# Experts split by token count: short ones in four 32-column tiles, the rest in two 64-column tiles

## The chip, the core and the metric

The kernel runs on one core of a Trainium2 chip. The metric is the device time of one execution in microseconds. The core has TensorE (matmuls; the profile's PE, its weight loads PEld), VectorE (DVE), ScalarE (ACT), GpSimd (POOL) and SyncE (SP), which here issues nearly all transfers from device memory to the on-chip memory.

## The reference, cut to what matters

One layer of a block for 256 latent tokens of width 1024. Its first half (a modulated input projection, three token mixers, a merge) is not touched. The second half is a mixture of 32 experts, of which each token uses 4:

```python
logits = (h @ w_router + b_router)                 # 256 x 32
top_val, top_idx = lax.top_k(logits, 4)
probs = softmax(top_val)                           # weight of a token at its experts
for each expert:
    gate, up = split(h @ w_gate_up + b_gate_up)    # 1024 -> 1024 and 1024
    gate = minimum(gate, 7); up = clip(up, -7, 7)
    y = ((up + 1) * gate * sigmoid(1.702 * gate)) @ w_down + b_down
    out += combine[:, expert, None] * y
```

and at the end a layer norm. All is float32. The weights of one expert are 12.6 MB, of all 403 MB.

## The kernel before, in words

**First part** (to about 310 us): the mixers, the merge, the router. It counts each expert's tokens into `cnt`, and the place of each token at each expert into `posq`.

**Experts.** The loop `for e in range(NE)` (L1479 to L1552) is unrolled in the program. For each expert 64 slots are filled: `select` (VectorE) makes the 0/1 matrix of tokens and slots, for two experts at a time, and `gather` (TensorE, then ScalarE) multiplies by it and writes the chosen tokens, transposed, into `hT`, half of the width at a time. `gate_up` (L1388) multiplies `hT` (64 columns, the stationary side) with 512 columns of weights at a time; two 64-column tiles of TensorE, `pg[0:64]` and `pg[64:128]`, work side by side. Each such float32 matmul is two matmul instructions in the profile. The columns of the weights are laid out in two halves (`hf`): the first half of gate and up is multiplied for all of the width (L1489), then `act` (L1395, five operations, four of them on VectorE) makes the gated product, while TensorE goes on with the second half (L1509, L1512). `spots` (L1373) makes the matrix `sT` that puts results back to their tokens, and the weights of the slots. `turn` (L1403) transposes the product, `down` (L1410) multiplies with the down weights, in two parts with a `turn` and a `gather` between. `spread` scales the result and splits it into a high and a low part, and `scatter` (L1421) adds both to the sums `acc` with `sT`; this happens in the next expert, after its first half of gates (L1492). `biases` writes the bias into a bank before the matmuls add to it, by a matrix `bse` that is copied from `bsel`.

**More than 64 tokens.** `cnt[e]` is loaded into a register of TensorE, VectorE and ScalarE. Two blocks under `tc.If(tv > SLOTS)` follow: `rest_gate` (L1503) does the first half for slots 65 to 128, with the gate weights still in place, and `rest` (L1518) all of the others. A block under `tc.If(most > 2 * SLOTS)` (L1557), behind the last expert, handles more than 128 tokens, which doesn't occur with these inputs. Where the condition is false the engine jumps over the block.

**Transfers.** `queue` holds all weights in order: for each expert four pieces of gate and up (`gu`) and two of down (`dn`), 2048 KB each; the last expert's down weights come in four of 1024 KB. On chip there are slots for nine pieces of 2048 KB. `pump` (L148) issues the queue's head on SP as soon as the text has a free slot; `done(key)` frees a slot and pumps. At run time the transfer waits on SP until the last reader of the slot that stands in the text before it is past. `done` of gate pieces 0 and 1 stands behind the block L1503, of 2 and 3 behind the block L1518, and of the down pieces each behind its part of `down`.

**End.** `stats3` and `norm2` (L1575 to L1600) normalise the sums and write four blocks of output. One of these goes through ScalarE and GpSimd (L1592 to L1594), and ScalarE issues its transfer (L1595).

The functions that the diff touches, with the line numbers of the profile:

Of the kernel before, what the change touches and what calls it, by code (L numbers as in the profile page):

```python
# [21 lines left out]
P = 128  # L22
# [95 lines left out]
def kernel(ctx, tc, x, cx, cols, rows, csts, wsm, wgt, bada, brt, sgub, bdn, bgu,  # L118
# [21 lines left out]
    for e in range(NE):  # L140
        queue += [(("gu", e, i), wgu[e, i]) for i in range(4)]
        if e < NE - 1:
            queue += [(("dn", e, i), wdn[e, i]) for i in range(2)]
        else:
            queue += [(("dn1", e, i), wdn[e, i // 2][:, 2048 * (i % 2):2048 * (i % 2) + 2048]) for i in range(4)]
    loaded = {}

    def pump():  # L148
        while queue:
# [11 lines left out]
            nc.sync.dma_start(out=s, in_=src)  # L161
# [63 lines left out]
    with ExitStack() as p1:  # L225
# [1058 lines left out]
        bsel = Buf(A2, NE, 2)  # L1284
# [20 lines left out]
        G.memset(bsel[:], 0.0)  # L1305
        for r in range(4):
            S.copy(out=bsel[32 * r:32 * r + 32, :, r % 2], in_=ident[32 * r:32 * r + 32, 32 * r:32 * r + 32])
# [33 lines left out]
    for t in range(2):  # L1341
        mm(ps[0:1, 64:64 + NE], ones[:, 0:1], sel[:, t], start=t == 0, stop=t == 1)


    def chunk():
        return dict(sT=Buf(R, 256), cwv=Buf(A2, 2), gT=Buf(A2, KB, SLOTS), gc=[Buf(A2, 256)])

    yhx, ylx = Buf(R, 512), Buf(R, 512)
    cur, over = chunk(), chunk()
    over["gc"] = over["gc"] + cur["gc"]  # L1350
    cur["gc"] = cur["gc"] + [Buf(A2, 256)]
    ysum = Buf(A2, 512)
    up, sg = ysum[:, 0:256], ysum[:, 256:512]
    sw = ysum[:, 0:256].rearrange("p (t a n) -> p t a n", t=2, a=2)
# [18 lines left out]
    def spots(b, sl, e):  # L1373
        for t in range(2):
            V.tensor_scalar_mul(sw[:, t], sl[:, t, :].unsqueeze(1).to_broadcast([P, 2, SLOTS]), cw[:, t, e:e + 1])
        pw = sps2()
        for t in range(2):
            T.transpose(pw[:, P * t:P * t + P], sw[:, t].rearrange("p a n -> p (a n)"), ident[:])  # L1378
# [3 lines left out]
    def bias_of(e):  # L1382
        V.tensor_copy(out=bse[e % 2][:].rearrange("p (q n) -> p q n", q=2), in_=bsel[:, e, :].unsqueeze(2).to_broadcast([P, 2, SLOTS]))  # L1383

    def biases(e, hf, pg):
        mm(pg[:], bse[e % 2][:], bst[:, hf, :], start=True, stop=False, skip_group_check=True)  # L1386

    def gate_up(hT, pg, ks, w):  # L1388
        for k in ks:
            wk = w[k // 2].rearrange("p (k n) -> p k n", k=2)  # L1390
            for q in range(2):
                mm(pg[64 * q:64 * q + 64, :], hT[:, k, :], wk[:, k % 2, 512 * q:512 * q + 512], start=False, stop=k == KB - 1,  # L1392
# [288 lines left out]
```

## Time and profile before

| | |
|---|---|
| median of 3 runs | 1283.39 us (1281.62 to 1283.76) |
| the profiled execution | 1286.55 us, of which the span is 1284.7 |
| TensorE busy | 1189.9 us |
| VectorE busy | 461.2 us |
| ScalarE busy | 284.5 us |
| moved from device memory | 468.92 MB |

A page of the profile shows busy time per engine and, in 40 slices, the share of busy time, the clock that TensorE was granted (1.00 is full speed) and the rate of the transfers. Times in the views count from the start of the span. "Idle before" is the time that the engine stood still ahead of an instruction, and behind the arrow stands what ended it; `PEq` is TensorE's sequencer, which runs branches and waits.

### The profile page before, as it was taken

The numbers are of one execution on the slowest core, as the hardware profiler recorded it, in microseconds if no ns is written. First come the engines' busy times: TensorE is split into PE (matmuls) and PEld (weight loads), VectorE is DVE, ScalarE is ACT, GpSimd is POOL, SyncE is SP. The second block draws the span as 40 slices with busy tenths as digits, with TensorE's granted clock in tenths as the row PEclk, the third lists the DMA queues.
The fourth block names the chain that finished last, engine by engine and source line by source line (L and its number), as shares of the span: only waits on it lengthen the run. The fifth ranks groups of instructions, "written<-read, shape, count | busy, mean of one in ns | idle before, by whom it ended". The sixth has DMA issues, their size and how long they took to land. (4 is left out here: it accounts for less than half of the span.)

```text
span 1284.7 us, 16504 instructions
## 1 busy us (share of the span) xinstructions
PE 1189.9 (93%) x6619; PEld 611.3 (48%) x6624; DVE 461.2 (36%) x988; ACT 284.5 (22%) x548; POOL 28.3 (2%) x42
## 2 busy tenths in 40 slices
PE   7997999999999999999999999999888999889884
PEld 5897889995333434334433334333333333333321
DVE  6488768796222222222212221222222122212223
ACT  5352745634111111111111111111111111111101
POOL 1000000002000000000000000000000000000000
PEclk9998999998999999999999999999999999999998
DMA  9745648777999999989959999999999999999993
GB/s 389 274 152 204 232 178 296 294 311 297 392 415 427 424 427 427 427 323 429 375 213 387 428 425 427 427 425 427 427 426 426 427 425 427 425 427 426 428 423 149
DMA packets 39470, 471.74 MB, mean 367 GB/s; under 512 B 4529, under 2 KB 4657, under 8 KB 7473
## 3 DMA queue, kind: packets, MB, share of 16 engines
q1 hardware_dynamic: 37008, 463.75, 87.3%
q10 hardware_dynamic: 1696, 4.40, 1.0%
q8 instruction: 89, 1.46, 0.5%
q0 software_dynamic: 640, 1.84, 0.5%
q14 instruction: 37, 0.30, 0.1%
HBM read 468.92 MB, written 1.05 MB: 366 GB/s over the span
## 5 line engine op out<-in xcount | busy, mean ns | idle before, releaser
L1392 PE MATMUL bank<-arena,arena 128*64 128x512 f32 x1808 | 408.8, 596 | 18.3 <-DMA arena<-in_wgu_dram 17.7
L1414 PE MATMUL bank<-arena,arena 128*64 128x512 f32 x1088 | 251.7, 604 | 25.5 <-DMA arena<-in_wdn_dram 17.9
L1392 PEld LDWEIGHTS bank<-arena,arena 128*64 128x64 f32 x1808 | 124.1, 137 | 260.5 <-issue 235.6
L1414 PEld LDWEIGHTS bank<-arena,arena 128*64 128x64 f32 x1088 | 79.3, 138 | 174.8 <-issue 152.7
L246 PE MATMUL bank<-rounded 128*128 128x256 f32 (+1 forms) x1152 | 149.6, 289 | 0.1
L246 PEld LDWEIGHTS bank<-rounded 128*128 128x128 f32 x1152 | 144.0, 195 | 1.8 <-issue 0.6
L1397 DVE TENSOR_SCALAR arena<-bank 128x256 f32<-128x256 f32 x68 | 28.9, 424 | 280.4 <-PE bank L1392 280.4
L1417 DVE SCALAR_TENSOR_TENSOR arena<-bank,arena,g2q 128x512 f32<-128x512 f32 x33 | 24.8, 751 | 271.8 <-PE bank L1414 163.3
L1398 ACT ACTIVATE arena<-arena 128x256 f32<-128x256 f32 x68 | 28.4, 417 | 366.5 <-DVE arena L1397 362.6
L1407 ACT COPY arena<-bank 128x256 f32<-128x256 f32 x68 | 25.3, 372 | 294.4 <-PE bank L1406 294.4
L1392 PE MATMUL bank<-arena 128*64 128x512 f32 x368 | 85.4, 606 | 3.0 <-DMA arena<-in_wgu_dram 2.6
L343 DVE TENSOR_TENSOR rounded<-arena,rounded 128x2048 fp32r<-128x2048 f32 x29 | 66.2, 2284 | 15.1 <-ACT rounded L338 15.1
L1367 PE MATMUL bank<-arena 128*128 128x128 f32 (+1 forms) x576 | 69.9, 275 | 0.7 <-DVE rounded L1383 0.7
L1367 PEld LDWEIGHTS bank<-arena 128*128 128x128 f32 x576 | 66.9, 192 | 1.5 <-ACT arena L1232 0.8
L1370 ACT ACTIVATE arena<-bank,shc 128x128 f32<-128x128 f32 (+1 forms) x144 | 53.3, 450 | 50.7 <-PE bank L1367 50.7
L338 ACT CAST rounded<-arena 128x2048 fp32r<-128x2048 f32 x29 | 55.0, 1898 | 9.2 <-PE bank L246 5.6
L1379 DVE TENSOR_SCALAR rounded<-bank 128x256 fp32r<-128x256 f32 x34 | 14.5, 425 | 117.0 <-PE bank L1378 117.0
L1392 PEld LDWEIGHTS bank<-arena 128*64 128x64 f32 x368 | 25.2, 139 | 53.6 <-issue 45.3
L1418 ACT CAST rounded<-arena 128x512 fp32r<-128x512 f32 x33 | 20.4, 618 | 111.5 <-DVE arena L1417 111.5
L1426 PE MATMUL bank<-rounded 64*128 64x512 f32 x264 | 40.8, 418 | 3.6 <-ACT rounded L1418 3.1
L1426 PEld LDWEIGHTS bank<-rounded 64*128 64x128 f32 x264 | 22.8, 184 | 33.9 <-issue 25.1
L1386 PE MATMUL bank<-rounded 128*128 128x512 f32 x68 | 32.5, 477 | 5.8 <-PEq L1503 3.8
(326 smaller groups left out, 889.5 us busy)
## 6 DMA issues: line engine op xcount, KB each, us to landing
arena<-in_wgu_dram SPq DMA_DIRECT2D x128, 2048.0 KB, 28.7
arena<-in_wdn_dram SPq DMA_DIRECT2D x62, 2048.0 KB, 27.3
arena<-in_win_dram SPq DMA_DIRECT2D x23, 1024.0 KB, 5.3
arena<-in_wada_dram SPq DMA_DIRECT2D x16, 1024.0 KB, 4.9
arena<-in_wad_dram SPq DMA_DIRECT2D x8, 1024.0 KB, 11.1
arena<-in_wbr_dram SPq DMA_DIRECT2D x4, 1024.0 KB, 5.6
arena<-in_wout_dram SPq DMA_DIRECT2D x4, 1024.0 KB, 5.5
arena<-in_wdn_dram SPq DMA_DIRECT2D x4, 1024.0 KB, 33.6
```

The source lines that it names most:

```text
L246: mm(o, l, r, start=start and n == 0, stop=stop and n == len(todo) - 1)
L338: S.copy(out=wh[:, 0:2048], in_=w)
L343: V.tensor_tensor(out=wl[:, 0:2048], in0=w, in1=wh[:, 0:2048].bitcast(F32), op=ALU.subtract)
L1367: mm(pg[:, w * k:w * k + w], h2[:, t, 512 * a + P * k:512 * a + P * k + P], b["sl"][:, t].rearrange("p i n -> p (i n)"), start=t == 0, sto ...
L1370: S.activation(out=b["hT"][:, 4 * a + k].rearrange("p i n -> p (i n)"), in_=pg[:, w * k:w * k + w], func=AF.Identity, scale=shc[:, 1, 4 * ...
L1386: mm(pg[:], bse[e % 2][:], bst[:, hf, :], start=True, stop=False, skip_group_check=True)
L1392: mm(pg[64 * q:64 * q + 64, :], hT[:, k, :], wk[:, k % 2, 512 * q:512 * q + 512], start=False, stop=k == KB - 1, skip_group_check=True)
L1397: V.tensor_scalar_min(gc[:], pg[:, 0:256], LIMIT)
L1398: S.activation(out=sg[:], in_=gc[:], func=AF.Sigmoid, scale=SW_ALPHA)
L1407: S.copy(out=b["gT"][:, 4 * hf:4 * hf + 4, :].rearrange("p (q j) n -> p j q n", q=2), in_=pt[:, 0:256].rearrange("p (j q n) -> p j q n", j ...
L1414: mm(py[64 * q:64 * q + 64, :], b["gT"][:, k, :], wk[:, k % 2, 512 * q:512 * q + 512], start=k == 0, stop=k == KB - 1)
L1426: mm(acc[t][hf][:], b["sT"][sl, P * t:P * t + P], y_[sl, :], start=False, stop=last and y_ is ylx, skip_group_check=True)
```

## The change

- **Weights by input block.** The gate and up weights of an expert are laid out so that each piece holds two blocks of 128 inputs, and each block all 2048 columns, as four quarters of 256 gate and 256 up columns. Before, a piece held one half of the columns for four blocks.
- **Branch per expert.** `by_count` puts the gate part and the down part each under `tc.If(tv > FEW)` with an else, FEW being 32; expert 0 always takes the wide side without a branch.
- **Short side.** `gate_up` puts 32 slots on four 32-column tiles, one quarter of the columns on each, 512 wide, all into one bank; one `act` follows instead of two, and one `turn`. `down` uses the four tiles for two halves of the output and two of the input; the two input halves are added by `scatter`, whose matrix `sT` has the 32 slots four times.
- **Wide side.** `gate_up_wide` does both halves for the first four input blocks, then both for the rest, into two banks. `spots` and both `act` come after it.
- **Order.** All gates of an expert now stand ahead of `scatter` of the expert before, of both overflow blocks and of the gathers; the down part comes last, in one go. `done` of all four gate pieces stands behind the second overflow block, `done` of both down pieces behind the down part.
- **Overflow.** The first block gathers and does the first half of the input blocks, the second block all the rest, down and scatter included. They have banks and buffers for both halves.
- **Biases.** `biases2` writes the bias for either case into the bank ahead of the branch, through two matrices whose content depends on the count; they are made once by small operations on GpSimd.
- **More than 128 tokens.** `many` stands before the last expert and loads the weights again.
- **Last expert and end.** Its last gate piece and its last down piece come in smaller transfers, and the output block of GpSimd is issued by SP instead of ScalarE.

The core of the diff (removed functions and small renames are left out):

```diff
-        queue += [(("gu", e, i), wgu[e, i]) for i in range(4)]
+        queue += [(("gu", e, i), wgu[e, i]) for i in range(4 if e < NE - 1 else 3)]
...
+            queue += [(("gu1", e, i), wgu[e, 3][:, 2048 * i:2048 * i + 2048]) for i in range(2)]
...
+            if key == ("dn1", NE - 1, 3):
+                for i in range(2):
+                    nc.sync.dma_start(out=s[:, 1024 * i:1024 * i + 1024], in_=src[:, 1024 * i:1024 * i + 1024])
...
+    for r in range(4):
+        for t in range(2):
+            mm(ps[32 * r:32 * r + 32, 128:129], sel[:, t], ones[:, 0:1], start=t == 0, stop=t == 1)
...
+    def biases2(e, pg):
+        biases(e, 0, pg)
+        mm(pg[:], bsx[e % 2][:], bst[:, 1, :], start=False, stop=False, skip_group_check=True)
+    def gate_up(hT, pg, w):
+        for k in range(KB):
+            for r in range(4):
+                mm(pg[FEW * r:FEW * r + FEW, :], hT[:, k, 0:FEW], w[k][:, 512 * r:512 * r + 512], start=False, stop=k == KB - 1,
+                   skip_group_check=True)
+    def gate_up_wide(hT, pgs, ks, w, between=None):
+        for hf in range(2):
+            if hf and between:
+                between()
+            for k, wk in zip(ks, w):
+                for q in range(2):
+                    mm(pgs[hf][64 * q:64 * q + 64, :], hT[:, k, :], wk[:, 1024 * hf + 512 * q:1024 * hf + 512 * q + 512], start=False,
+                       stop=k == KB - 1, skip_group_check=True)
+    def down(b, py, w):
+        for i in range(4):
+            for h in range(2):
+                for q in range(2):
+                    mm(py[64 * q + FEW * h:64 * q + FEW * h + FEW, :], b["gT"][:, 2 * i + h, 0:FEW],
+                       w[i][:, D * h + 512 * q:D * h + 512 * q + 512], start=i == 0, stop=i == 3)
...
+        def gates(small):
+            shares(sl[:, :, 0:FEW] if small else sl, e)
+            if small:
+                gate_up(hT, g0, w)
+            else:
+                gate_up_wide(hT, [g0, g1], range(4), w, lambda: biases(e, 1, g1))
+                gate_up_wide(hT, [g0, g1], range(4, KB), w[4:])
+            pw = spots()
+            act(cur["gc"][0], g0)
+            places(cur, pw)
+            if not small:
+                act(cur["gc"][1], g1)
+        def downs(small):
+            turn(cur, 0, 4 if small else 2)
+            (down if small else down_wide)(cur, g0, wd)
+        by_count(gates)
+        if 0 < e < NE - 1:
+            scatter(prev, yx)
...
         with tc.If(tv > SLOTS):
-            rest_gate(e, w)
+            over_begin(e, 1, [g0, g1])
+            for hf in range(2):
+                biases(e, hf, (g0, g1)[hf])
+            over_gates([g0, g1], range(4), w)
+        if e % 2 == 0 and e + 2 < NE:
+            select(q_["sl"][:], 2, 0, e + 2)
+        if e % 2 == 0 and e + 2 < NE:
+            gather(q_, 0, 2)
         with tc.If(tv > SLOTS):
-            rest(e, g1, wu, wd)
+            over_gates([g0, g1], range(4, KB), w[4:])
+            over_end([g0, g1])
+            turn(over, 0)
+            py = sps2()
+            down_wide(over, py, wd)
+            spread(over, py, yx)
+            scatter(over, yx)
+        if e % 2 and e + 1 < NE:
+            gather(q_, 1, 2)
+        for key in [("gu", e, i) for i in range(4)] if not last else [...]:
+            done(key)
...
+            bias_of(e + 1)
+        if e + 2 < NE:
+            biases2(e + 1, g1)
+        by_count(downs)
+        for key in [("dn", e, i) for i in range(2)] if not last else [("dn1", e, i) for i in range(4)]:
             done(key)
...
-    S.dma_start(out=out[0:P, 512:1024], in_=o[0][1])
     stats3(1, 1)
     norm2(0, 0)
+    nc.sync.dma_start(out=out[0:P, 512:1024], in_=o[0][1])
...
-    gu = gu.transpose(0, 5, 1, 3, 2, 6, 4, 7).reshape(NE, 4, 2, P, 2048).transpose(0, 1, 3, 2, 4).reshape(NE, 4, P, 4096)
+    gu = A(w_gate_up)[0].reshape(NE, 4, 2, P, 2, 4, 256).transpose(0, 1, 3, 2, 5, 4, 6).reshape(NE, 4, P, 4096)
```

## Rows read from the trace of the kernel before

**Rows 1.** Page, transfer rate in 40 slices of 32.1 us.
```profile
GB/s 389 274 152 204 232 178 296 294 311 297 392 415 427 424 427 427 427 323 429 375 213 387 428 425 427 427 425 427 427 426 426 427 425 427 425 427 426 428 423 149
```

**Rows 2.** Windows: start:end length, engines' busy us (instructions), PEclk, DMA share, GB/s.
```profile
316.00:324.00 8.00, 7.84 (x39) 2.47 (x37) 3.81 (x12) 2.70 (x4) 0.00 (x0) 1.00 0.24 63
...
330.00:384.00 54.00, 51.22 (x250) 20.36 (x251) 12.97 (x34) 7.16 (x18) 0.00 (x0) 0.97 1.00 414
...
550.00:584.00 34.00, 33.53 (x174) 14.02 (x173) 6.65 (x17) 5.57 (x14) 0.00 (x0) 1.00 0.84 329
...
628.00:644.00 16.00, 15.51 (x72) 5.12 (x70) 5.21 (x14) 1.47 (x4) 0.00 (x0) 1.00 0.72 280
...
644.00:700.00 56.00, 53.27 (x255) 20.41 (x253) 11.43 (x27) 7.60 (x18) 0.00 (x0) 0.97 0.75 294
...
700.00:1254.00 554.00, 509.29 (x2475) 195.46 (x2471) 126.58 (x323) 69.21 (x168) 0.00 (x0) 1.00 1.01 426
```

**Rows 3.** Waits of SP's queue: us in total, times, longest.
```profile
SPq L161 <- PEq L1503: 200.5, 29, 12.8
...
SPq L161 <- PEq L1518: 166.2, 28, 7.5
```

**Rows 4.** Timeline of SP: start us, us, engine line op out<-in.
```profile
321.34 0.33 SPq L161 DMA_DIRECT2D arena<-in_wgu_dram  x1
```

**Rows 5.** DMA issues from 321.2 to 321.5: KB each, us to landing.
```profile
arena<-in_wgu_dram SPq DMA_DIRECT2D x1, 2048.0 KB, 7.7
```

**Rows 6.** Timeline of TensorE, expert 3; in brackets idle before, and releaser.
```profile
397.19 7.04 PE L1392 MATMUL bank<-arena,arena 128*64 128x512 f32 x32
...
404.16 1.20 PE L1426 MATMUL bank<-rounded 64*128 64x512 f32 x8
...
405.52 0.47 PE L1386 MATMUL bank<-rounded 128*128 128x512 f32 x1 [0.17 <-PEq L1503]
...
414.06 3.65 PE L1414 MATMUL bank<-arena,arena 128*64 128x512 f32 x16 [0.31 <-PEq L1518]
...
417.92 1.95 PE L1367 MATMUL bank<-arena 128*128 128x128 f32 x16
...
423.52 1.89 PE L1392 MATMUL bank<-arena 128*64 128x512 f32 x8
```

**Rows 7.** Timeline of TensorE, first instructions of experts 10 and 11.
```profile
612.38 3.60 PE L1392 MATMUL bank<-arena 128*64 128x512 f32 x16
...
671.14 1.45 PE L1392 MATMUL bank<-arena,arena 128*64 128x512 f32 x5
```

**Rows 8.** Timeline of TensorE at 17 us: 128x32 column tiles.
```profile
17.00 1.07 PE L260 MATMUL bank<-arena 128*32 128x256 f32 x16 [0.92 <-ACT arena L298]
```

**Rows 9.** Timeline of VectorE: one activation of a gate half.
```profile
1248.19 0.42 DVE L1397 TENSOR_SCALAR arena<-bank 128x256 f32<-128x256 f32 x1 [7.32 <-PE bank L1392]
...
1249.63 0.42 DVE L1401 SCALAR_TENSOR_TENSOR arena<-arena 128x256 f32<-128x256 f32 x1
```

**Rows 10.** Timeline of all engines, the tail.
```profile
1262.76 3.65 PE L1414 MATMUL bank<-arena,arena 128*64 128x512 f32 x16 [0.46 <-ACT arena L1407]
...
1267.27 1.99 PE L1444 MATMUL bank<-arena,rounded 64*128 64x512 f32 x8 [0.85 <-DVE arena L1543]
...
1271.19 1.29 DVE L1576 BATCH_NORM_STATS2 st<-bank 128x6 f32<-128x512 f32 x2 [3.97 <-PEq L1557]
...
1275.10 1.61 DVE L1584 SCALAR_TENSOR_TENSOR arena<-arena,rsx 128x512 f32<-128x512 f32 x1
...
1278.27 0.29 ACT L1579 ACTIVATE rsx<-mvx,lneps 128x1 f32<-128x1 f32 x1 [3.86 <-POOL arena L1594]
```

**Rows 11.** DMA issues from 1234.6 to 1234.8: the last weights.
```profile
arena<-in_wdn_dram SPq DMA_DIRECT2D x1, 1024.0 KB, 29.4
```

**Rows 12.** Timeline of TensorE, and the window around the instruction.
```profile
991.35 5.25 PE L1414 MATMUL bank<-arena,arena 128*64 128x512 f32 x16 [2.28 <-DMA arena<-in_wdn_dram]
...
990.00:996.60 6.60, 5.25 (x17) 1.67 (x18) 1.41 (x4) 0.05 (x1) 0.00 (x0) 0.74 1.02 429
```

More of the change, by code (lines that the diff above doesn't have):

```diff
@@ L1283 @@
         bse = [Buf(R, P) for _ in range(2)]
-        bsel = Buf(A2, NE, 2)
+        bsx = [Buf(R, P) for _ in range(2)]
+        bsel, bselx = Buf(A2, NE, 4), Buf(A2, NE, 4)
+        few = Buf(A2, 2, NE)
         alid = Buf(A2, P)
@@ L1424, in scatter, with scatter_whole @@
                 sl = slice(64 * hf, 64 * hf + 64)
[L1425 to L1440 removed]
+                for y_ in y:
+                    mm(acc[t][hf][:], b["sT"][sl, P * t:P * t + P], y_[sl, :], start=False, stop=False, skip_group_check=True)
+    def scatter_whole(b, last):
         for t in range(2):
@@ L1443, in scatter_whole @@
                 sl = slice(64 * hf, 64 * hf + 64)
-                mm(acc[t][hf][:], b["sT"][sl, P * t:P * t + P].bitcast(F32), y[sl, :], start=False, stop=last, skip_group_check=True)
-    def rest(e, g, wu, wd, end=False):
-        turn(over, 0)
-        biases(e, 1, g)
-        gate_up(over["hT"][:, :, 0, :], g, range(8), wu)
-        act(over, 1, g)
-        py = sps2()
-        down(over, py, range(4), wd)
-        turn(over, 1)
-        down(over, py, range(4, 8), wd)
-        if end:
-            V.scalar_tensor_tensor(out=ysum[:], in0=py[:], scalar=over["cwv"][:, 0:1], in1=g2q[:], op0=ALU.mult, op1=ALU.mult)
-            scatter_whole(over, ysum, False)
-        else:
-            spread(over, py)
-            scatter(over)
+                mm(acc[t][hf][:], b["sT"][sl, P * t:P * t + P].bitcast(F32), ysum[sl, :], start=False, stop=last, skip_group_check=True)
@@ L1478 @@
     eq.free()
+    for r in range(4):
+        rs = slice(32 * r, 32 * r + 32)
+        G.tensor_tensor(out=few[rs, 1], in0=ident[rs, rs], in1=few[rs, 0, 0:1].to_broadcast([32, NE]), op=ALU.mult)
+        G.tensor_copy(out=bselx[rs, :, 2 + r % 2], in_=few[rs, 1])
+        if r % 2:
+            G.tensor_copy(out=bsel[rs, :, 1], in_=few[rs, 1])
+        for j in (2, 3) if r % 2 else (1,):
+            G.tensor_tensor(out=bsel[rs, :, j], in0=bsel[rs, :, j], in1=few[rs, 1], op=ALU.subtract)
     for e in range(NE):
+        last = e == NE - 1
         p = pair[e // 2 % 2]
@@ L1522 @@
+        if e % 2 and e + 1 < NE:
+            gather(q_, 1, 2)
+        for key in [("gu", e, i) for i in range(4)] if not last else [("gu", e, 0), ("gu", e, 1), ("gu", e, 2), ("gu1", e, 0), ("gu1", e, 1)]:
+            done(key)
         if e + 1 < NE:
             bias_of(e + 1)
-        if e % 2 == 0 and e + 2 < NE:
-            select(q_["sl"][:], 2, 0, e + 2)
-        down(cur, g0, range(4), wd)
-        for key in [("dn", e, 0)] if e < NE - 1 else [("dn1", e, 0), ("dn1", e, 1)]:
+        if e + 2 < NE:
+            biases2(e + 1, g1)
@@ L1528 @@
+        by_count(downs)
+        for key in [("dn", e, i) for i in range(2)] if not last else [("dn1", e, i) for i in range(4)]:
             done(key)
-        turn(cur, 1)
-        if e + 2 - e % 2 < NE:
-            gather(q_, e % 2, 2)
-        if e + 1 < NE:
-            biases(e + 1, 0, g1)
-        down(cur, g0, range(4, 8), wd)
-        for key in [("dn", e, 1)] if e < NE - 1 else [("dn1", e, 2), ("dn1", e, 3)]:
-            done(key)
-        if e < NE - 1:
-            spread(cur, g0)
+        if not last:
+            spread(cur, g0, yx)
```

216 lines of the change are left out of this document (117 added, 99 removed).

## The prediction, on record before the result

> **What bounds the kernel now.** I read the profile in four steps. First the page: its transfer rate runs at about 427 GB/s through nearly all of the last 30 slices, with two dips in the middle [rows 1]. Second, the stretches that split the expert stage at those dips [rows 2]; TensorE shows as busy in and beside the dips (33.53 us of 34 in one, 509.29 of 554 after the last), so busy shares alone don't say who waits. A stretch at 63 GB/s for 8 us has lost 8 x (1 - 63/427) = 6.8 us of transfer. The same sum gives 1.6 us for 330 to 384, 7.8 for 550 to 584, 5.5 for 628 to 644 and 17.4 for 644 to 700: 39.1 us in all. From 700 to 1254 the rate is 426 GB/s: nothing that TensorE does there can shorten the time, because weights come at the queue's full rate. Third, what the queue waits for in those dips: a free buffer. There are nine buffers of 2048 KB, an expert needs six, and the queue's longest waits in total end at TensorE's skip of the two overflow blocks (L1503, L1518) [rows 3]. Fourth, one release in detail: TensorE reaches L1503 of expert 0 and SP issues the next piece at 321.34, at the end of expert 0's first half of gates [rows 4]; a piece issued into an empty queue lands 7.7 us later [rows 5].
>
> So the end is set by the transfers plus the tail, and the length of the transfers is 2.097 MB / 427 GB/s = 4.9 us a piece plus the time in which all nine buffers are held. The changed program must be judged by when it gives buffers back, not by how busy TensorE is.
>
> **A recurrence for both kernels.** Piece n lands at the later of (landing of n-1) + 4.97 and (release of piece n-9) + 7.7. The 4.97 is an estimate: 4.91 by the rate above, plus a little for bias and code traffic, set so that the kernel before comes out. I ran it over 32 experts with TensorE's times below. Routing the reference's own inputs gives the tokens of the experts: 17 34 33 47 48 4 19 77 8 46 101 48 28 12 11 40 25 1 46 42 36 8 28 31 44 14 21 64 12 39 32 8. Experts 7 and 10 overflow 64 slots, which is where the dips are; 17 have up to 32, of which expert 0 runs wide anyway. For before, an expert takes TensorE 423.52 - 397.19 = 26.3 us [rows 6] and an overflow expert 671.14 - 612.38 = 58.8 us [rows 7]. The recurrence then loses 39.2 us to held buffers, where the stretches show 39.1, so I trust it to a few us.
>
> **The change part by part.**
>
> *Short experts.* The nearest row to 128x32 tiles of four is the modulation projection: sixteen instructions of 256 columns in 1.07 us [rows 8], that is four groups of four, each about 0.215 us after a first latency. At 512 columns four instructions take 0.43 us, so 64 gate instructions take 6.9 us instead of 13.7 (64 x 0.2135 from 3.65 for 16 [rows 6]) and the 32 of the down projection 3.4 instead of 6.8. Saved: 10 us of TensorE in each of 16 experts, 160 us. Nearly all of it lies under transfers: a small expert needs about 18 us where its weights need 29.8. On the path it only serves to catch up after a long expert.
>
> *Wide experts.* The columns cost the same. What moves is the order. Before, the gate half's activation, the turn and the gather lay among matmuls. Now all gates come first, then spots, the scatter of the previous expert (1.20), two skips, the gather (1.95), two bias matmuls (0.95) and the downs. In even experts the gather waits for a select that stands behind the whole chain on VectorE, whose one activation runs from 1248.19 to 1250.05 [rows 9]. I get 14.4 us to the end of the gates and 14.6 (odd) or 16.5 (even) after them: 30 us against 26.3 now, no longer below 29.8 of transfer. Experts 1 to 4 are all wide, so nothing is caught up before expert 5.
>
> *Release of buffers.* This decides. The overflow blocks still read the gate weights, so all four pieces stay held until the skips, which now stand behind all gates. Expert 0: gates from 314.1 to 328.5, first two pieces free at 329.3, where now it is 321.3. The queue has been empty since about 317, so this costs 8.0 us, and piece 15 (behind expert 1) another 2.4. Later, with TensorE in step, five further buffers cover 24.8 us and a normal expert stalls nothing.
>
> *Overflow experts.* The extra work is the same (about 33 us), but the downs, and with them the two down pieces, come after the entire overflow, gather and biases. Expert 7: last gate piece lands at 518.7, gates end 524.1, overflow gates 547, downs 572.6. Piece 55 waits for that and lands 12.0 us late; before, this expert lost 7.8 by the stretches. Expert 10 then follows one small and one wide expert, which give back only 11 us: stalls 5.4 + 15.8 + 6.5 = 27.7 against 5.5 + 17.4 = 22.9. Sum of all held time after: 15.0 + 2.4 + 0.3 + 12.0 + 27.7 = 57.4 us, against 39.2: **+18.2 us**.
>
> *Branches.* Each expert has two more, with a join for TensorE. A skip costs 0.17 us at L1503 and 0.31 at L1518 [rows 6]; I take 0.2 for each of five per expert. At 0 the sum above is +14.1, at 0.5 it is +26.9. The upper end of what this trace shows is the branch over the last block: 1269.26 to 1271.19, 1.9 us [rows 10]. I take the near rows because the new blocks are of the size of those.
>
> *Set-up.* Eight more one-column matmuls, some 16 small POOL operations and one compare before expert 0; the gather of the first pair waits for VectorE anyway. The POOL results are first wanted for expert 1, some 20 us later. 0 to 1 us. More code is fetched through the same queue: 0 to 3 us, I take 1.
>
> *Tail.* The last weights land at 1234.72 + 29.4 = 1264.1 [rows 11], and the span ends at 1284.7: 20.6 us. Expert 31 has 8 tokens. After its last half piece four instructions remain, about 1.1 us, instead of 2.3 (to 1266.41). The branch over the rare block moves ahead of the expert: 1.9 saved. The output of the first half no longer holds ScalarE, whose square root waited until 1278.27 behind POOL; VectorE then ends about 1.2 us sooner (four operations of 0.75 right after 1276.7, some slowed beside POOL as the 1.61 was) [rows 10]. Saved 1.2 + 1.9 + 1.2, less 0.3 for the new join and 0.5 for broadcast rows that are now loaded beside the last weights: 3.5 us; bounds 0 and 5.
>
> A slower clock is the doubt here. After an idle 2.28 us, sixteen matmuls took 5.25 us instead of 3.65 [rows 12]: the granted clock of that stretch is 0.74 in the mean, so it fell from 2.4 to 1.2 GHz and rose again within one burst. Small experts leave about 3 us idle a piece (4.9 less 1.9). At half speed a piece takes 3.4 us, still under 4.9, so the transfers hide it; in the tail 3.1 us of matmuls would take 1.4 to 3.1 more. The Trainium skill's "TensorE: Matmul & The Clock Gate", section "HAM oscillation", says that matmul bursts with waits for DMA between them run at the throttled clock; this burst agrees, while the stretch from 700 to 1254 as a whole was granted 1.00 [rows 2]. By that rule the tail keeps about 0.4 of its 3.5 us; by the mostly full clock in 700 to 1254, it keeps all of it.
>
> Sum: +18.2 + 1 - 3.5 = +15.7 us. The profiled execution took 1286.55 (span 1284.7 and 1.9 around it), so it would take 1302.3; the median of the runs is 3.2 below it, hence 1299.
>
> **Rivals.**
>
> *Faster: the short experts keep TensorE in step.* If TensorE is in step again before expert 10, that expert loses only what expert 7 lost before (7.8, not 22.9): 15 us less, and expert 7 no more than it did. With +10.8 at the start, 1 for code and -3.5 in the tail: -6.8, or 1276.6. It decides if experts 8 and 9 give back over 22 us; for it: TensorE has 10 us less to do in expert 8. Against: expert 9 has 46 tokens, and the downs of expert 10 still hold two buffers to the end.
>
> *No change: buffers are given back at the last read, not at the skip.* The overflow reads in expert 10 do release within the block. Then the start costs nothing and the recurrence gives +5.6, with code and tail +3.1: 1286.5, at the edge of what can be told. Against: SP waits 29 and 28 times for exactly the skips [rows 3].
>
> *Branches cost far more.* At 1 us a join, halfway up to 1.9, the recurrence gives +43, hence about 1324. The Trainium skill's "Runtime: NRT & Kernel Launch", section "Instruction fetch mechanics", says that a taken branch to code outside the fetched pages waits for a fetch. By that rule this is the case if the alternatives are too long for what is held; the skips in this trace, over blocks of about this length, took 0.31 us.
>
> *It doesn't do what it says:* four tiles run no faster than two pairs. Then small experts gain nothing while all experts have the new order: +40 by the recurrence, about 1320. Against: rows 8.
>
> **How the numbers follow.** Forecast 0.64, faster rival 0.14, no change 0.12, branches 0.06, tiles 0.04. About 0.2% (2.6 us) is what a measurement of this kernel can tell from no change. The no-change rival is spread over both sides of that edge. Faster: 0.14 and a little of the second, 0.16. Same: 0.08 from the second and 0.01 of the forecast's low end, 0.09. Slower: 0.75. The forecast's own range is 1290 (joins at 0, best tail) to 1311 (joins at 0.5, no tail gain, code 3 us). With the cases below it down to 1278 about 2 in 10 are left out.
>
> **What would show it.** Right: the dip at 316 to 324 lasts to about 331; the transfer rate falls to near 0 again within 555 to 580 and 640 to 705; from 715 on it is 426 without a dip while TensorE is idle 3 us a piece in short experts; the stretch from last landing to end is about 17 us. Wrong: no deeper dip at the start (release is finer), dips gone around expert 10 (in step), a granted clock near half for long stretches with TensorE late for the transfers, or waits at the new joins above 0.5 us.

## The result: 1339.22 us, 4.4% slower

The kernel after takes 1339.22 us (1331.92 to 1343.23) against 1282.51 us for the kernel before: ratio 1.0438 [1.0389, 1.0487]. The sign was forecast, the size was not: 1299 was predicted, and 1311 was the top of the range. The profiled execution took 1343.23 us, its span 1341.2.

The page first: transfer rate and granted clock in 40 slices, now of 33.5 us, to lay beside [rows 1].

```profile
PEclk9998999998898998898989888988998899898977
...
GB/s 391 249 181 213 206 204 330 229 373 201 379 402 350 410 427 426 384 204 407 324 251 181 427 425 426 425 426 426 426 427 424 426 427 426 425 428 423 427 413 135
```

The rate is full at the end as before, and the dips lie in the same part, deeper and wider. The clock line says something new: it is below 9 in many slices, where the kernel before has:

```profile
PEclk9998999998999999999999999999999999999998
```

The same stretches as in [rows 2], and the rest of the expert stage (start:end length, busy us of PE, PEld, DVE, ACT, POOL with instructions, PEclk, DMA share, GB/s):

```profile
316.00:324.00 8.00, 8.00 (x39) 2.58 (x37) 2.00 (x7) 1.86 (x3) 0.00 (x0) 1.00 0.00 0
324.00:330.00 6.00, 4.59 (x22) 1.36 (x18) 2.98 (x8) 0.61 (x2) 0.00 (x0) 1.00 0.14 30
330.00:384.00 54.00, 47.03 (x211) 19.63 (x212) 9.60 (x26) 6.68 (x17) 0.00 (x0) 0.91 0.95 391
550.00:584.00 34.00, 28.43 (x134) 11.15 (x132) 5.60 (x14) 3.85 (x10) 0.00 (x0) 0.95 0.64 264
644.00:700.00 56.00, 51.78 (x233) 22.67 (x231) 10.62 (x28) 7.01 (x19) 0.00 (x0) 0.88 0.70 292
750.00:1254.00 504.00, 384.56 (x2198) 149.72 (x2190) 92.62 (x243) 54.01 (x132) 0.00 (x0) 0.91 1.01 426
```

From 750 on the transfers run at 426 GB/s, as they did from 700 in [rows 2]. Nearly all that was lost was lost before, some 4 us behind it and 1.4 in the tail. The landing of each weight piece says where: the table sums, in us, by how much a piece landed later than 4.97 us after the one before it (pieces less than 0.6 us late are left out). The rightmost two columns belong to experiments below.

| pieces | before | after | e13 | e15 |
|---|---|---|---|---|
| 9 (first release) | 7.0 | 15.3 | 16.2 | 4.3 |
| 10 to 53 | 3.5 | 15.9 | 3.0 | 16.7 |
| 54 to 63 (behind expert 7) | 6.4 | 19.7 | 13.9 | 11.0 |
| 64 to 76 (behind expert 10) | 22.8 | 41.4 | 24.1 | 25.8 |
| 77 to 185 | 4.7 | 8.3 | 10.5 | 10.2 |
| sum | 44.4 | 100.6 | 67.7 | 68.0 |
| last landing | 1264.1 | 1319.2 | 1285.5 | 1283.3 |
| landing to end | 20.6 | 22.0 | 14.8 | 17.9 |

What SP's queue waits for (us in total, times, longest) is what [rows 3] showed, the skip of an overflow block, now L1615; the first release, in [rows 4] at 321.34, is issued at 328.71:

```profile
SPq L166 <- PEq L1615: 415.0, 29, 20.9
```
```profile
328.71 0.33 SPq L166 DMA_DIRECT2D arena<-in_wgu_dram  x1
```

TensorE in the turn of wide expert 3, to lay beside [rows 6] (start, us, in brackets idle before and what ended it):

```profile
411.81 5.33 PE L1427 MATMUL bank<-arena,arena 128*64 128x512 f32 x16 [0.22 <-issue]
...
417.50 10.52 PE L1427 MATMUL bank<-arena,arena 128*64 128x512 f32 x48
...
428.32 1.19 PE L1475 MATMUL bank<-rounded 64*128 64x512 f32 x8
431.46 3.00 PE L1378 MATMUL bank<-arena 128*128 128x128 f32 x16 [1.95 <-DVEq L1624]
...
436.37 3.66 PE L1459 MATMUL bank<-arena,arena 128*64 128x512 f32 x16 [0.64 <-ACT arena L1442]
...
444.34 1.89 PE L1427 MATMUL bank<-arena 128*64 128x512 f32 x8
```

The turn takes 444.34 - 411.81 = 32.5 us. The gather (L1378) waits 1.95 us until VectorE has come to the second skip (L1624), then runs slower, 3.00 us where [rows 6] has 1.95; the granted clock from 431.4 to 434.5 is 0.65 in the mean. A short expert, number 6, and the first gates of expert 7 behind it:

```profile
498.62 7.05 PE L1417 MATMUL bank<-arena,arena 128*32 128x512 f32 x64
...
509.00 2.02 PE L1378 MATMUL bank<-arena 128*128 128x128 f32 x16 [1.82 <-DVE arena L1370]
...
515.80 0.66 PE L1441 MATMUL bank<-ident,arena 128*128 128x128 f32 x2 [3.93 <-issue]
516.97 5.64 PE L1450 MATMUL bank<-arena,arena 128*32 128x512 f32 x32 [0.51 <-ACT arena L1442]
522.53 1.94 PE L1427 MATMUL bank<-arena 128*64 128x512 f32 x8
```

Four tiles run at once as forecast: 64 gate instructions in 7.05 us. But the turn takes 23.9 us, with 3.93 us of "issue" behind the second branch by count, where TensorE waits for nothing that these rows show (e8 comes back to it). Over the whole run (waits of TensorE: us in total, times, longest):

```profile
PE bank L1378 <- DVEq L1624: 49.3, 25, 3.3
...
PE bank L1441 <- issue: 28.8, 9, 4.2
...
PE bank L1407 <- PEq L1510: 5.1, 1, 5.1
```

The third is in the tail, against [rows 10]:

```profile
1305.22 0.77 PE L1407 MATMUL bank<-rounded 128*128 128x512 f32 x1 [5.12 <-PEq L1510]
...
1311.21 5.74 PE L1417 MATMUL bank<-arena,arena 128*32 128x512 f32 x45
...
1321.21 6.29 PE L1450 MATMUL bank<-arena,arena 128*32 128x512 f32 x32 [0.51 <-ACT arena L1442]
...
1332.85 0.29 ACT L1670 ACTIVATE rsx<-mvx,lneps 128x1 f32<-128x1 f32 x1
```

While TensorE stood 5.12 us at the branch over the block for more than 128 tokens (L1510), the last expert's gate pieces came in; its down projection then began 2 us behind the last landing. ScalarE's square root is no longer held by POOL: it starts at 1332.85, 0.24 us after VectorE began the last step of the statistics that it reads.

### The profile page after: what moved, and what is told of

It is laid out like the page before. It is cut to its first block, busy times and chain, and to the rows that moved or that the text cites. A ratio compares the mean times of both kernels' runs of the same rounds, so it can differ in the third digit from the quotient of the medians.

```text
span 1341.2 us, 16594 instructions
## 1 busy us (share of the span) xinstructions
PE 1104.3 (82%) x6623; PEld 581.5 (43%) x6623; DVE 429.0 (32%) x927; ACT 270.5 (20%) x516; POOL 31.9 (2%) x59
## 5 line engine op out<-in xcount | busy, mean ns | idle before, releaser
L1427 PE MATMUL bank<-arena,arena 128*64 128x512 f32 x976 | 222.5, 603 | 11.3 <-DMA arena<-in_wgu_dram 11.1
L1459 PE MATMUL bank<-arena,arena 128*64 128x512 f32 x576 | 137.9, 623 | 28.4 <-ACT arena L1442 24.2
L1378 PE MATMUL bank<-arena 128*128 128x128 f32 (+1 forms) x576 | 94.1, 333 | 56.9 <-DVEq L1624 49.3
L1427 PEld LDWEIGHTS bank<-arena,arena 128*64 128x64 f32 x976 | 68.7, 139 | 152.9 <-issue 134.1
L1417 PE MATMUL bank<-arena,arena 128*32 128x512 f32 x832 | 109.8, 644 | 30.6 <-DMA arena<-in_wgu_dram 29.8
L1431 DVE TENSOR_SCALAR arena<-bank 128x256 f32<-128x256 f32 x52 | 21.9, 422 | 331.8 <-PE bank L1427 184.3
L1378 PEld LDWEIGHTS bank<-arena 128*128 128x128 f32 x576 | 87.7, 242 | 70.5 <-issue 63.9
L1432 ACT ACTIVATE arena<-arena 128x256 f32<-128x256 f32 x52 | 21.7, 418 | 436.9 <-DVE arena L1431 436.9
L1450 PE MATMUL bank<-arena,arena 128*32 128x512 f32 x512 | 82.5, 767 | 14.3 <-ACT arena L1442 11.8
L1459 PEld LDWEIGHTS bank<-arena,arena 128*64 128x64 f32 x576 | 40.4, 142 | 103.3 <-issue 70.4
L1417 PEld LDWEIGHTS bank<-arena,arena 128*32 128x32 f32 x832 | 28.8, 115 | 105.9 <-issue 59.6
L1441 PE MATMUL bank<-ident,arena 128*128 128x128 f32 x104 | 23.8, 311 | 32.7 <-issue 28.8
L1450 PEld LDWEIGHTS bank<-arena,arena 128*32 128x32 f32 x512 | 19.6, 135 | 69.1 <-issue 50.0
L1427 PE MATMUL bank<-arena 128*64 128x512 f32 x176 | 44.3, 626 | 0.0
## 6 DMA issues: line engine op xcount, KB each, us to landing
arena<-in_wdn_dram SPq DMA_DIRECT2D x62, 2048.0 KB, 25.8
```

Of the source, the lines that this page charges most:

```text
L1378: mm(pg[:, w * k:w * k + w], h2[:, t, 512 * a + P * k:512 * a + P * k + P], b["sl"][:, t].rearrange("p i n -> p (i n)"), start=t == 0, sto ...
L1417: mm(pg[FEW * r:FEW * r + FEW, :], hT[:, k, 0:FEW], w[k][:, 512 * r:512 * r + 512], start=False, stop=k == KB - 1, skip_group_check=True)
L1427: mm(pgs[hf][64 * q:64 * q + 64, :], hT[:, k, :], wk[:, 1024 * hf + 512 * q:1024 * hf + 512 * q + 512], start=False, stop=k == KB - 1, ski ...
L1441: T.transpose(pt[:, P * j:P * j + P], b["gc"][hf][:, P * j:P * j + P], ident[:])
L1450: mm(py[64 * q + FEW * h:64 * q + FEW * h + FEW, :], b["gT"][:, 2 * i + h, 0:FEW], w[i][:, D * h + 512 * q:D * h + 512 * q + 512], start=i ...
L1459: mm(py[64 * q:64 * q + 64, :], b["gT"][:, 2 * i + h, :], w[i][:, D * h + 512 * q:D * h + 512 * q + 512], start=i + h == 0, stop=i + h == 4)
```

## The experiments

Theory: the loss is TensorE's own time per turn (waits on VectorE behind the gates, the half clock behind these waits, code behind a jump), which gives buffers back later. Rivals: the clock alone, the later release in itself, the overflow experts' long turn alone. Ratios are to the kernel before, on the same chip.

**e1, the clock.** Matmuls on zeros in front of both waits keep TensorE at work.
```diff
+        if e < NE - 1:
+            idle2(acc[0][0][:], 8)
...
+        if e < NE - 1:
+            idle2(acc[0][0][:], 6)
         by_count(downs)
```


> The changed kernel with idle matmuls on zeros: 8 ahead of the first overflow block, 6 ahead of the down branch (experts 0 to 30). They fill the waits in which the clock falls and cost some 1.3 us an expert where nothing is waited for. Theory clock (bursts after waits of 2 us at half speed make experts 0 to 10 late, and that is what the held buffers cost): granted clock in 316 to 750 from 0.92 to near 1.00, time 8 to 15 us less, 1324 to 1331. Theory waits (the gaps themselves cost, the clock is a side effect): clock up, time the same or up to 10 us more, 1339 to 1349.

Measured: 1332.92, ratio 1.0364 [1.0346, 1.0382]. The clock did return (from 0.91 in the kernel after to 1.00 in this window), the transfers did not move (399 GB/s in both):
```profile
330.00:550.00 220.00, 197.05 (x1062) 79.62 (x1077) 44.83 (x119) 27.33 (x68) 0.00 (x0) 1.00 0.96 399
```
By the ratios this gives 0.7% of the time, some 9 us (the two intervals allow about 0.2 to 1.3%); the time itself lies between the ranges of the two theories. It is rather a lower bound for the clock, since the idle matmuls take time too, 1.3 us an expert by the expectation. Most of the loss is left, so the clock is not the main cause.

**e2, the gather alone moved.**
```diff
-        if e % 2 == 0 and e + 2 < NE:
-            gather(q_, 0, 2)
...
-        if e % 2 and e + 1 < NE:
-            gather(q_, 1, 2)
...
         by_count(downs)
+        if e + 2 - e % 2 < NE:
+            gather(q_, e % 2, 2)
```


> The changed kernel with both gathers moved behind the down part, so TensorE no longer waits for VectorE to pass the second overflow block, and gate pieces 2 and 3 are released some 4 us earlier. Theory waits (49 us in 25 waits at the gather, 11 of them ahead of the last dip): 15 to 25 us less, 1314 to 1324, dips shorter. Theory code fetch (what follows a jump waits 3 to 5 us whatever stands ahead of it): the wait moves to the turn of the down part; under 8 us less, 1331 or more.

Measured: 1336.01, 1.0390 [1.0373, 1.0407]. The wait went on to the bias matmul, whose operand VectorE makes behind the same chain:
```profile
PE bank L1407 <- DVE rounded L1404: 60.8, 27, 3.6
```
The interval overlaps that of the kernel after. So moving one instruction is no test of the wait: the next one that depends on VectorE inherits it.

**e3, no short sides.**
```diff
-    V.tensor_scalar(out=few[:, 0, 0:1], in0=ps[:, 128:129], scalar1=float(FEW), scalar2=None, op0=ALU.is_le)
+    V.tensor_scalar(out=few[:, 0, 0:1], in0=ps[:, 128:129], scalar1=0.0, scalar2=None, op0=ALU.is_le)
...
-            with tc.If(tv > FEW) as cmp:
-                part(False)
-            with cmp.Else():
-                part(True)
+            part(False)
```


> The changed kernel without the branch by count: every expert takes the two 64-column tiles, all else in place. Theory of the prediction (short sides help only to catch up, experts 5, 6 and 8): those three take 31 instead of 24 us and later ones 30.5 to 31 against 29.8 of transfer: 10 to 35 us more, 1350 to 1375. Theory branch (the two branches per expert and the fetch behind them cost more than the short sides give): 1325 to 1339.

Measured: 1399.71, 1.0872 [1.0833, 1.0910], above the ranges of both theories (1375 at most). Within the new order the short sides are worth 4% of the time. Without them TensorE falls behind the transfers late too (403 GB/s here, 426 in the kernel after):
```profile
750.00:1290.00 540.00, 475.25 (x2244) 192.54 (x2244) 109.19 (x284) 63.97 (x159) 0.00 (x0) 0.96 0.97 403
```

**e4 and e9, the rare block's branch,** taken out of the kernel after and of the kernel before.
```diff
-        with tc.If(most > 2 * SLOTS):
+        if False:
```
(The load of the count `most` goes too; in the kernel before the two lines stand four columns further left.)

> The changed kernel without the block for more than 128 tokens (no expert has that many here) and its branch. In the tail TensorE waited 5.1 us there while three gate pieces of the last expert lay ready. Theory tail (that wait makes TensorE late for the last weights): last matmul 5 to 7 us earlier, stretch from last landing to the end 22 to 15 or 17 us, time 1332 to 1335. Theory clock in the tail (the last expert runs at half speed anyway): 2 us or less, 1337 or more.

> The kernel before without the block for experts of more than 128 tokens and its branch (it isn't entered with these tokens). Theory (the tail loses to that branch wherever TensorE has to pass it late): 2 to 5 us below before, since it stands behind the last expert there and only the output follows. Rival (the branch costs only where the last expert's gates queue behind it, as in the kernel after): within 1.5 us of before. It is the fair yardstick for e4 and e5, which leave out the same block.

Measured: e4 1331.30, 1.0354 [1.0336, 1.0372], with 15.7 us from last landing to end instead of 22.0; e9 1280.45, 0.9969 [0.9956, 0.9982]. The branch costs both kernels: some 4 us before; after, 8 by the medians and 11 by the ratios, of which the tail shows 6.

**e5, nothing that waits for VectorE behind the gates.** As e4, and:
```diff
+        if e + 1 < NE:
+            bias_of(e + 1)
+        if e % 2 == 0 and e + 2 < NE:
+            select(q_["sl"][:], 2, 0, e + 2)
         by_count(gates)
         if 0 < e < NE - 1:
             scatter(prev, yx)
+        if e + 2 - e % 2 < NE:
+            gather(q_, e % 2, 2)
...
-        over["hT"] = q_["hT"][:, 4:8]...
+        over["hT"] = (p if e % 2 else q_)["hT"][:, 4:8]...
```
(The three calls at their old places go.)

> As e4_no_rare_block (the block for more than 128 tokens left out), and in every turn the next expert's bias matmul and selection stand ahead of its gates' branch, its gather right behind the scatter and ahead of the first overflow block, so that TensorE meets nothing behind its gates that waits for VectorE. Theory (the waits of some 2 us a turn at the gather, and the half clock behind them, make the experts longer than forecast): some 15 to 19 us below e4, 1312 to 1316 us, wide experts about 30 us on TensorE, and the clock of the first 750 us near 1.00. Rival (the waits only move to the next thing that depends on VectorE, as in e2): 1328 us or more, with a wait of about 2 us a turn at another line.

Measured: 1300.48, 1.0126 [1.0101, 1.0150]; e4 and e5 differ by 2.3% of the time, some 29 us, more than the theory's 15 to 19.

**e6 and e7, both kernels without overflow blocks** (slots above 64 of an expert are left out).
```diff
-        with tc.If(tv > SLOTS):
-            over_begin(e, 1, [g0, g1])
...
-        with tc.If(tv > SLOTS):
-            over_gates([g0, g1], range(4, KB), w[4:])
...
```
```diff
-        with tc.If(tv > SLOTS):
-            rest_gate(e, w)
...
-        with tc.If(tv > SLOTS):
-            rest(e, g1, wu, wd)
```

> The kernel after without both overflow blocks (slots above 64 of an expert are left out). Theory (short sides are worth their time, but held buffers are set by the start and the turn of a wide expert too): about 58 us below the kernel after, 1280 us, still 20 to 40 us above e7. Rival (all that the change costs comes by the long turn of the overflow expert): within 10 us of e7, about 1250.

> The kernel before without its overflow blocks (slots above 64 left out): the yardstick for e6. 25 to 37 us below the kernel before, 1249 to 1261 us, since the landings that wait for buffers in expert 8's turn come at once.

Measured: e6 1251.39, 0.9743 [0.9718, 0.9767]; e7 1244.42, 0.9687 [0.9663, 0.9711]. The rival of e6 holds: without these blocks the change costs only 0.6%. They cost 3.1% of the time in the kernel before and 7.0% in the kernel after, skipped and taken together; e6 can't tell the two apart. The window that lost most is then full (292 GB/s in the kernel after):
```profile
644.00:700.00 56.00, 39.33 (x258) 13.78 (x258) 9.13 (x25) 5.99 (x15) 0.00 (x0) 0.88 1.01 427
```

**e8, the small side's code first.**
```diff
-            with tc.If(tv > FEW) as cmp:
-                part(False)
+            with tc.If(tv < FEW + 1) as cmp:
+                part(True)
             with cmp.Else():
-                part(True)
+                part(False)
```


> As after, but with the small side's code standing first and the wide one in the branch's other arm. Theory (the 3 to 4 us that TensorE waits at the first matmul behind the down part of a small expert are the fetch of code that lies beyond the block jumped over): these waits go from the small experts 5 to 7 to wide ones, 0 to 15 us below or above after, with a wait of 3 to 4 us put down to issue in wide turns. Rival (the wait belongs to the short run of work, not to the jump): the small experts keep their 22 to 25 us and after's time stands within 0.3%.

Measured: 1332.31, 1.0360 [1.0328, 1.0393], which touches the interval of the kernel after. The short experts 5 and 6 take 19.8 and 19.3 us instead of 22.6 and 23.9, and have no such wait; here expert 5:
```profile
495.53 0.38 PE L1441 MATMUL bank<-ident,arena 128*128 128x128 f32 x2
497.14 3.64 PE L1450 MATMUL bank<-arena,arena 128*32 128x512 f32 x32 [1.23 <-ACT arena L1442]
```
The wide experts 2 to 4 take 37.8, 33.2 and 34.9 us instead of 34.0, 32.5 and 31.7 (expert 1: 30.8 instead of 31.5). But the waits of 3 to 4 us that the theory looks for there are not found: the longest put down to issue in these turns is 1.95 us, in expert 4. So the wait is not bound to the short run of work, and that the order of the two arms decides is not shown. It goes without a change of order too: in e15 the arms stand as in e5, and the waits at L1441 and L1450 put down to issue are 1.8 us in all, where e5 has 27.5.

What TensorE waits for is in the trace. In each of the nine waits of the kernel after a packet of 16 KB of code (DMA queue q8, kind "instruction") arrives, and the matmul starts 1.4 to 1.7 us behind it; in the eleven of 0.9 us or more in e5 it is 1.3 to 1.7 us. In the wait of expert 6, from 511.87 to 515.80, the packet runs from 513.16 to 514.24 (window 513.0 to 514.3: queue, kind, packets, MB, share):
```profile
q8 instruction: 1, 0.02, 5.2%
```

**e10, e11, e13, e14: the repaired order with nothing left out.** e10 is e5 with the rare block back and e8's order of sides; the last scatter stands behind the rare block:
```diff
-            scatter(prev, yx)
             room = many([g0, g1])
+            scatter(prev, yx)
```


> The order of e5 with nothing left out: the block for more than 128 tokens is back, ahead of the last scatter of expert 30 instead of behind it, and the small side's code stands first, as in e8. Theory: e5's time and 0 to 5 us for the rare branch, less up to 5 us for the two waits of 3.3 us at small experts 5 and 6 that e5 still shows: 1296 to 1305 us, still 0.8 to 1.6% above before. Rival (small first moves its fetch into wide turns, where more buffers wait): 1308 us or more.

Measured: 1320.62, 1.0274 [1.0254, 1.0293], 16 us above the theory's range and within the rival's: a wait at the gather was back, in 25 turns, 32.7 us in all.
```profile
361.29 2.05 PE L1378 MATMUL bank<-arena 128*128 128x128 f32 x16 [1.47 <-DVEq L1621]
```

e11 is e10 with scatter and gather behind the first overflow block.
```diff
-        if 0 < e < NE - 1:
-            scatter(prev, yx)
-        if e + 2 - e % 2 < NE:
-            gather(q_, e % 2, 2)
...
             over_gates([g0, g1], range(4), w)
+        if 0 < e < NE - 1:
+            scatter(prev, yx)
+        if e + 2 - e % 2 < NE:
+            gather(q_, e % 2, 2)
         with tc.If(tv > SLOTS):
```

> As e10, but the first overflow block stands right behind the gates, ahead of scatter and gather, so that the buffers of the first two gate pieces come free 3.2 us earlier. Theory (what is left against before are buffers held at pieces 9, 57 and 75, each waiting for the first branch behind the gates): 5 to 8 us below e10. Rival (TensorE meets VectorE's pass of the branch at the gather again): within 2 us of e10, with waits of 1 to 2 us a turn at the gather.

Measured: 1337.35, 1.0405 [1.0390, 1.0420], 17 us above e10; neither theory. The waits of the gather stay (27.7 us in 24 turns) and long ones behind the jumps come to wide turns too: 3.34 us in expert 3, whose turn takes 36.8 us.

e13 is e10 without e8's edit, so the wide side stands first again; e14 is e10 with one line more.
```diff
         if e + 2 - e % 2 < NE:
+            sps2()
             gather(q_, e % 2, 2)
```


> e10 with the wide side's code first again, as in the kernel after and in e5; nothing is left out. Theory (with the small side first, the gather's bank is the one that the small side's selection was transposed into, so the gather waits until VectorE has passed the whole wide side, 1.47 us a turn in e10; with the wide side first it waits only for the read of that bank): 12 to 20 us below e10, 1302 to 1309 us, no wait of 1.5 us at the gather, wide experts 28.5 us on TensorE. Rival (the block for more than 128 tokens, not the order of the sides, made e10 slower than e5): within 5 us of e10.

> e10 with one change: the gather takes the other of the two PSUM banks that rotate. Theory (it is the bank): the wait of 1.47 us a turn at the gather goes in wide turns, and the time falls by 10 us or more to 1301 to 1310 us. Rival (it is the order of the two arms in code, whatever the bank): within 4 us of e10.

Measured: e13 1301.46, 1.0117 [1.0100, 1.0134]; e14 1309.77, 1.0188 [1.0171, 1.0205]. Both as the theory has it: the line that turns the two PSUM banks by one takes 11 us away, and with it the wait. The other 8 us between e14 and e13 come with the order of the arms; what does it wasn't tried. The gather in e14:
```profile
359.72 2.05 PE L1378 MATMUL bank<-arena 128*128 128x128 f32 x16
```
The rare block's branch still holds TensorE 5.2 us in e13, now ahead of the last scatter, and costs nothing that shows against e5. Expert 3 in e13:
```profile
403.26 3.65 PE L1427 MATMUL bank<-arena,arena 128*64 128x512 f32 x16 [0.20 <-issue]
...
407.27 10.52 PE L1427 MATMUL bank<-arena,arena 128*64 128x512 f32 x48
...
419.23 2.05 PE L1378 MATMUL bank<-arena 128*128 128x128 f32 x16
421.86 0.47 PE L1407 MATMUL bank<-rounded 128*128 128x512 f32 x1 [0.58 <-PEq L1626]
...
431.80 1.89 PE L1427 MATMUL bank<-arena 128*64 128x512 f32 x8
```
28.5 us from gates to gates, 4 less than in the kernel after. The five wide experts 0 to 4 take 27.3, 28.5, 32.1, 28.5 and 30.3.

**e15, the first release.**
```diff
+        if e:
             with tc.If(tv > SLOTS):
                 over_begin(e, 1, [g0, g1])
...
```


> e5 (no block above 128 tokens) without the overflow blocks of expert 0 alone (its slots above 64 are left out; it has 17 tokens, so they are empty here). Theory (what is left of e5's loss against e9 begins at the start: all four gate pieces of expert 0 are held until its first overflow branch is passed, 9 us later than before): the stall at piece 9 falls from 16.1 to 4 to 6 us and the time by 6 to 11 us, to 1290 to 1295. Rival (a later stall takes up what is won, since the next pieces wait for TensorE anyway): less than 3 us below e5.

Measured: 1303.07, 1.0139 [1.0122, 1.0156], not below e5. The dip at the start is gone (30 GB/s in the kernel after), and the stretch behind it falls from 391 to 357:
```profile
324.00:330.00 6.00, 6.00 (x38) 3.38 (x35) 3.34 (x9) 0.99 (x3) 0.00 (x0) 1.00 1.02 437
330.00:384.00 54.00, 50.49 (x242) 18.33 (x240) 11.64 (x33) 6.71 (x17) 0.00 (x0) 1.00 0.86 357
```
The table shows the same: piece 9 gains 12 us, pieces 10 to 53 lose 14. A release is only worth what TensorE's pace behind it keeps up. The waits for code, gone here (e8), don't show in the time either.

**e12, the change's output part alone, in the kernel before:** the quarter of the output that ScalarE sent goes by SyncE.
```diff
-    S.dma_start(out=out[0:P, 512:1024], in_=o[0][1])
     stats3(1, 1)
     norm2(0, 0)
+    nc.sync.dma_start(out=out[0:P, 512:1024], in_=o[0][1])
```

> The kernel before with only the output part of the change: the quarter of the output that ScalarE sends goes out by SyncE, behind the first quarter. Theory: 0 to 2 us below before (the last stores leave some 1 us earlier, since ScalarE's last normalisation no longer stands behind its own transfer's issue). Rival: no difference that can be measured, within 0.1%.

Measured: 1282.35, 0.9975 [0.9963, 0.9986], which is faster than both kernels. ScalarE's square root follows the statistics at once; in [rows 10] it waited for POOL until 1278.27:
```profile
1268.59 0.21 DVE L1578 BATCH_NORM_AGGREGATE mvx<-st 128x2 f32<-128x12 f32 x1
1268.72 0.75 DVE L1583 SCALAR_TENSOR_TENSOR arena<-bank,mvx,arena 128x512 f32<-128x512 f32 x1
1268.84 0.29 ACT L1579 ACTIVATE rsx<-mvx,lneps 128x1 f32<-128x1 f32 x1
```

## Why the prediction was wrong in size

In profiled executions the forecast was 1302.3 and the run 1343.2: 40.9 us apart. The last landing moved by 55.1 us against 18.2 + 1 forecast, a miss of 35.9; the tail by +1.4 against -3.5, a miss of 4.9.

**The step that failed** is the one on the length of TensorE's turns: "14.6 (odd) or 16.5 (even) after them: 30 us", "a small expert needs about 18 us", an overflow expert at 33 us more than a wide one, and the branches at 0.2 us a join. Those times are sums of instructions, with VectorE waited for in even turns only. By them experts 0 to 10 take 6 x 30 + 3 x 18 + 2 x 63 = 360 us. Measured are 401.8 (from 313.7 to 715.5), 42 more: 13 in the six wide experts (30.9 to 34.0 each), 18 in the three short ones (22.6 to 25.4) and 11 in the two overflow experts (67.1 and 69.6). As before the change, TensorE gives buffers back only as its turn proceeds, so a longer turn makes later pieces land late until the transfers are in step, at 750. With it fell "a normal expert stalls nothing": the forecast's held time was 15.0 us at piece 9, 2.4 and 0.3 between it and expert 7, 12.0 behind expert 7 and 27.7 behind expert 10; the table has 15.3, 15.9, 19.7 and 41.4. What the sum left out:

- TensorE waits for VectorE in odd turns too: at the gather 22.3 us in experts 0 to 10, of which 9.5 in odd ones. The places, the second half's activation and the skip itself lie on VectorE between the gates and everything TensorE may do next. Taking this away, with the rare block's branch where it does no harm, gives 1301.46 in e13: 3.2% less of the time by the ratios, some 41 us (38 by the medians), of which up to 0.8% is that branch (e4). Experts 0 to 10 then take 364.4 us.
- The clock behind the waits is within it. In expert 10 of the kernel after and of e13 (columns as in the windows above) the same 275 matmul instructions take 8.3 us less at the full clock:
```profile
645.90:715.50 69.60, 62.66 (x275) 26.48 (x273) 12.33 (x32) 8.37 (x22) 0.00 (x0) 0.88 0.58 236
620.20:679.80 59.60, 54.34 (x275) 22.49 (x273) 12.33 (x32) 8.38 (x22) 0.00 (x0) 1.00 0.83 341
```
- A jump can cost far more than a skip: nine waits of 2.1 to 4.2 us at the second branch by count, 28.8 us in all, where the forecast had 0.2 us for each join. Only three of them, 10.8 us in experts 5, 6 and 8, come before 750, where they count. The rival "branches cost far more" had 1 us at each of five joins of every expert, which is not what happened; few jumps cost much. The Trainium skill's "Runtime: NRT & Kernel Launch", section "Instruction fetch mechanics", says that a taken branch to code outside the fetched pages waits for a fetch of it; the trace agrees, with a packet of code 1.4 to 1.7 us ahead of the end of each wait. Why some jumps wait and others don't stays open.
- The tail. "Saved 1.9" for the rare block's branch was a loss: moved ahead of the last expert it held TensorE 5.1 us, and without it the tail is 6 us shorter (e4). The output part did give its gain (e12: 0.25% [0.14, 0.37], some 3 us; 1.2 forecast). The doubt on the clock was right: the last 32 matmuls took 6.29 us, where e8's row above has 3.64.

**What held.** The view of the kernel: judged by when buffers come free, not by TensorE's busy share. The start of the dip (329.3 forecast, 328.71 measured) and its size (15.0, 15.3). The large stalls behind expert 0, 7 and 10, and full rate behind them (from 750; 715 forecast), but not the 15.9 us at pieces 10 to 53. Four tiles at once. The rivals "faster" and "buffers given back at the last read" failed: SP's queue waits at L1615 for 415 us. Of the signs of being wrong, waits at the new joins above 0.5 us came true. And the recurrence: that it gave 39.2 for the kernel before is no test, since its 4.97 was set to that end, but e13 is one. With turns of 360 us it puts the last landing 18.2 + 1 us behind 1264.1, at 1283.3; in e13, with 364.4, it is 1285.5. The 1 us for more code is of the right size, though code has queues of its own on the profile's page (q8 and q14): 1.76 MB before and 2.21 after, at 427 GB/s an estimate of 1.1 us.

**What stays open.** e13 is still 1.2% behind the kernel before. The table puts it at the pieces behind expert 0 (9 us) and expert 7 (7.5) and, behind 750, at pieces 77 to 185 (6), with 6 us won back in the tail; but e15 shows that a stall taken from one place comes back in the next. Whether the wide turn (27.3 to 32.1 against 26.3 to 28.7) or the down pieces held through the overflow turn weighs more wasn't tried apart.

## What to carry over

When a kernel is bound by transfers into few buffers, cost a reordering by what each engine has left to do while it waits: put the work that depends on nothing behind the step whose result takes longest, and look at what the next instruction in line needs before moving one. A skip that is already in the trace (0.17 and 0.31 us here) is no price for a new branch: what counted was whether TensorE had to wait for code behind it, and what lay ready meanwhile. Engine time saved where transfers decide buys little: without the overflow blocks both kernels end within 0.6% of each other (e6, e7), though half the experts of one take TensorE far less work. It bought 4% only where turns had become longer than the transfers (e3).

## What the hardware showed that was not expected

- With waits of about 2 us for VectorE in each turn the granted clock was 0.91 in 330 to 550, against 1.00 with idle matmuls in them (e1). "TensorE: Matmul & The Clock Gate" of the Trainium skill, section "HAM oscillation", tells of it with waits for DMA; here the waits were for VectorE.
- Which of two PSUM banks an instruction takes decided some 11 us (e10, e14). In e10 the gather takes the bank into which the short side transposes its places, and it waits in wide turns too, until VectorE has come through the branch by count to the next one (L1621).
- A jump held TensorE 2 to 4 us in some places, until 1.3 to 1.7 us after a 16 KB packet of code had arrived, and 0.58 us in others (the overflow skips of expert 3 in e13). Which jumps wait moved with edits far from them: 27.5 us of such waits in e5 became 1.8 in e15, which lacks only the overflow blocks of expert 0.
